# Feed-forward input stage: result banks and product banks of PSUM swap roles from block to block, weights split 2048 columns at a time, seven products at the 3rd and 6th pair

## The chip, the cores and the metric

The kernel runs on one core of a Trainium2 chip. Five engines work side by side, each through its own list of instructions in order: TensorE (PE, and PEld for the loading of its stationary operand), VectorE (DVE), ScalarE (ACT), GpSimd (POOL) and SyncE (SP), which here issues nearly all DMAs. Matrix products are summed in PSUM, eight banks of 128 partitions x 512 float32 values. The metric is the device time of one execution in microseconds (us); a run is the median of repeated executions.

## What is computed

One decoder layer for 256 tokens of width 2048: projections, two attention mixers, gates, an output product and a LayerNorm, then a feed-forward layer and a second LayerNorm. The change acts in the first half of the feed-forward layer, and in the names of the tiles elsewhere:

```python
FFN_HIDDEN = 5632

def _swiglu(h, w_ffn_in, w_ffn_out):
    g, u = jnp.split(h @ w_ffn_in, 2, axis=-1)
    return (jax.nn.silu(g) * u) @ w_ffn_out

h = _layer_norm(DEEPNORM_ALPHA * h + mix, ln1_g, ln1_b)
h = _layer_norm(DEEPNORM_ALPHA * h + _swiglu(h, w_ffn_in, w_ffn_out), ln2_g, ln2_b)
```

## The kernel before, in words

Every float32 operand is split into two parts of type float32r, a high one and a low rest (`split`, L70: a cast on ACT at L71, then a subtraction on DVE at L72), and each product is made of three matmuls (`mm3`, L90 to L93): high by high, high row by low weight, low row by high weight. Weights come in tiles of 128 x 2048 (1 MB, one DMA, three buffers called `raw`) and are split in halves of 1024 columns into two rings of eight buffers, `wh` and `wl`.

The feed-forward input product, h @ w_ffn_in, goes in 11 blocks `j` of 512 gate columns and 512 up columns. Block 0 is made in another way. Blocks 1 to 10 are made by `pair_product`: the 2048 rows of the weight are taken in eight pairs of 128-row tiles, and a pair is one `raw_fp` tile with four pieces of 512 columns (b11, b21 for the gate, b22, b12 for up). An ordinary pair gives 24 matmuls into four result banks, c11, c12, c21, c22 (gate and up, for the first and the second 128 tokens; in the trace `acc_fg` and `acc_fu`). In blocks 1 to 9 two of the pairs, those in `SEVEN`, are made by a Strassen-Winograd scheme: seven products instead of eight, so 21 matmuls. The first nine need the pieces b11, b21, b22 split (`whfp_2g`, `whfp_2u` and so on); the other twelve need four sums and differences of the pieces, which DVE makes in place (L737 to L740) and which are then split again (`whfp_2t`). Four of the seven products are shared between results and are summed in four further banks, `ps_` (`p` in the trace).

A scheduler sets the order of instructions on each engine from its own estimate of times; what each engine waits for follows from that order, since every engine works through its list in turn. The PSUM pool has two tags of four banks, `acc` and `tmp`. Before the change the four results of every block are `acc` and the four shared products are `tmp`. At the end of block j DVE adds shared products and results (L758 to L761) into SBUF, ACT and DVE form silu(gate) * up (L774, L775, L787), and two transposes on DVE write `rt` (L264). Eight steps later `move_blocks` (L286) copies `rt` to `act` with 16 DMAs of 32 x 256, issued by SP, the engine that also issues the `raw_fp` loads (L697). The first result bank of block j+1 is the bank that the add at L758 reads.

A `raw_fp` tile is free for a later load when its last split is done: the load of a pair takes the buffer of the pair three places earlier.

Of the kernel before, what the change touches and what calls it, by code (L numbers as in the profile page):

```python
# [17 lines left out]
P = 128  # L18
# [11 lines left out]
N = 512  # L30
# [14 lines left out]
def decoder_block(ctx, tc, xT, x, wz, lam_qk, subln, wa, wb, wo, g1, b1, b1T, wf, wfp, wfo, g2, b2,  # L45
# [24 lines left out]
    def split(src, hi, lo, eng=None):  # L70
        nc.scalar.copy(hi, src)  # L71
        (eng or nc.vector).tensor_sub(lo, src, hi)  # L72


    def split_weights(part, name, eng=None):
        wh = wp.tile([P, 2, N], F32R, tag="wh", name="wh" + name)
        wl = wp.tile([P, 2, N], F32R, tag="wl", name="wl" + name)
        split(part.rearrange("p (a n) -> p a n", n=N), wh, wl, eng)
        return wh, wl

    def weights(src, name, loads=1, pool=()):
        raw = wp.tile([P, 2048], F32, tag="raw", name="raw_" + name, bufs=3)
# [88 lines left out]
    def weights_and_x(src, name):  # L171
        c = int(name.split("_")[-1])
        for i in range(2):
            k0 = 4 * c + 2 * i
            raw = wp.tile([P, 2, N], F32, tag="raw", name="raw%d_%s" % (i, name), bufs=3)
            sv = src[:, i * 1024:(i + 1) * 1024].rearrange("p (a n) -> p a n", n=N)
            if k0 == 0:
                wh = wp.tile([P, 2, N], F32R, tag="wh", name="whf")
                wl = wp.tile([P, 2, N], F32R, tag="wl", name="wlf")
                xss = []  # L180
                for a in range(2):
                    xss.append(x_part(a, 1))
                    nc.sync.dma_start(raw[:, a, :], sv[:, a, :])
                for a in range(2):
                    split_x(xss[a], a, 1)
                    split(raw[:, a, :], wh[:, a, :], wl[:, a, :])
                yield wh, wl
            else:
                xs = x_part(k0, 2)
                nc.sync.dma_start(raw, sv)  # L190
                split_x(xs, k0, 2)
                yield split_weights(raw.rearrange("p a n -> p (a n)"), "%d_%s" % (i, name))
# [477 lines left out]

    SEVEN = (2, 4)
    forms = []

    def row_forms():
# [22 lines left out]

    def halves(src, name):  # L700
        n = src.shape[1]
        wh = wp.tile([P, 2, N], F32R, tag="wh", name="wh" + name)
        wl = wp.tile([P, 2, N], F32R, tag="wl", name="wl" + name)
        split(src, wh[:, 0:n], wl[:, 0:n])
        return [(wh[:, a, :], wl[:, a, :]) for a in range(n)]


    def pair_product(j):
        nk = KD // 2
        seven = SEVEN if j < NB_F - 1 else ()  # L710
        c11, c12, c21, c22 = [acc("acc_f%s_%d" % (c, j)) for c in ("g0", "u0", "g1", "u1")]
        ps_ = {}
        for i in range(nk):
            nm = "fp%d_%d" % (j, i)
            raw = load_pair(j, i)
            k0, k1 = 2 * i, 2 * i + 1
            first, final = i == 0, i == nk - 1
            if i not in seven:
                b11, b21 = halves(raw[:, 0:2], nm + "g")
                b22, b12 = halves(raw[:, 2:4], nm + "u")  # L720
                for ac, m, w0, w1 in ((c11, 0, b11, b21), (c12, 0, b12, b22), (c21, 1, b11, b21), (c22, 1, b12, b22)):
                    mm3(ac, *stat_h(m, k0), *w0, first, False)
                    mm3(ac, *stat_h(m, k1), *w1, False, final)
                tick()
                tick()
                continue
            n = seven.index(i)
            s0, s1 = n == 0, n == len(seven) - 1
            if s0:
                for f in (1, 6, 7, 5):  # L730
                    ps_[f] = tmp("p%d_%d" % (f, j))
            b11, b21 = halves(raw[:, 0:2], nm + "g")
            b22, = halves(raw[:, 2:3], nm + "u")
            mm3(ps_[1], *stat_h(0, k0), *b11, s0, s1)
            mm3(c11, *stat_h(0, k1), *b21, False, False)
            mm3(c12, *stat_s(4, n), *b22, False, False)
            nc.vector.tensor_sub(raw[:, 2], raw[:, 2], raw[:, 3])  # L737
            nc.vector.tensor_sub(raw[:, 3], raw[:, 3], raw[:, 0])
            nc.vector.tensor_add(raw[:, 0], raw[:, 2], raw[:, 0])
            nc.vector.tensor_sub(raw[:, 1], raw[:, 1], raw[:, 0])  # L740
            t2, t4 = halves(raw[:, 0:2], nm + "t2")
            t3, t1 = halves(raw[:, 2:4], nm + "t3")
            tick()
            mm3(ps_[6], *stat_s(2, n), *t2, s0, s1)
            mm3(ps_[7], *stat_s(3, n), *t3, s0, s1)
            mm3(ps_[5], *stat_s(1, n), *t1, s0, s1)
            mm3(c21, *stat_h(1, k1), *t4, False, False)
            tick()
            if s1:
                p1, u2, u3, t = [scr("%s_%d" % (c, j)) for c in ("p1", "u2", "u3", "u4")]  # L750
                nc.scalar.copy(p1, ps_[1])
                nc.vector.tensor_add(u3, p1, ps_[6])
                nc.vector.tensor_add(u2, u3, ps_[7])
                nc.vector.tensor_add(u3, u3, ps_[5])
                nc.vector.tensor_add(t, u2, ps_[5])
# [234 lines left out]
```

## Time and profile before

| what | value |
|---|---|
| time, median of 3 runs | 1380.2 us (1379.7 to 1380.85) |
| the profiled execution, its own time | 1384.11 us |
| its span, first to last instruction | 1382.3 us |
| granted TensorE clock, mean | 0.998 |
| PE busy | 1365.0 us, 99% of the span |
| DVE busy | 916.9 us, 66% |
| ACT busy | 644.5 us, 47% |
| DMA mean rate | 202 GB/s |

The busy share of PE counts a matmul from its start to its modelled end, and matmuls overlap: a 128 x 512 matmul lasts 0.39 us in the timeline, while the next one starts 0.23 us after it. Whether PE loses time is therefore read from the distances between starts, and from the time that a block of equal work takes. Below, T stands for the start of the first matmul of a block, and all times in a block are counted from it.

### The profile page before, as it was taken

The page shows a single profiled execution, that of the slowest core. Times are in us where ns is not written, and L with a number is a line of the kernel's source. Part 1 is how long each engine was busy: PE and PEld are TensorE (multiplying, and loading weights), DVE is VectorE, ACT ScalarE, POOL GpSimd, SP SyncE. Part 2 cuts the span into 40 slices and gives each one's busy share as a digit, 9 for nine tenths or more (in the row PEclk, how much of TensorE's full clock was granted, in tenths as well). Part 3 has the DMA queues.
Part 4 walks back from the last instruction along what each step waited for, and adds up shares of the span by engine and source line. Part 5 has one row for each costly group of instructions (what it writes and reads, how often), then busy time and mean ns, then how long its engine had stood idle before and what let it go on. Part 6 is the DMA issues. An engine that isn't in the chain of part 4 may idle for free.

```text
span 1382.3 us, 16276 instructions
## 1 busy us (share of the span) xinstructions
PE 1365.0 (99%) x6110; PEld 1126.0 (81%) x6110; DVE 916.9 (66%) x1161; ACT 644.5 (47%) x866; POOL 57.2 (4%) x64
## 2 busy tenths in 40 slices
PE   8999999999999999999999999999999999999997
PEld 6888888888888888888888888888788788888886
DVE  6666566766645454575878888888787765554555
ACT  4463444546444434443644455445454444444441
POOL 0001010100000000100000000000000000000003
PEclk9999999999999999999999999999999999999999
DMA  8583645464454649663445664546745676555541
GB/s 281 192 302 145 223 166 198 179 217 152 156 225 162 249 138 356 221 244 122 161 161 192 248 244 182 195 171 247 254 170 195 230 280 225 206 186 191 205 152 61
DMA packets 57151, 279.45 MB, mean 202 GB/s; under 512 B 10224, under 2 KB 22640, under 8 KB 25712
## 3 DMA queue, kind: packets, MB, share of 16 engines
q1 hardware_dynamic: 56784, 278.08, 55.2%
q8 instruction: 48, 0.79, 0.2%
q10 hardware_dynamic: 288, 0.33, 0.1%
q14 instruction: 31, 0.25, 0.1%
HBM read 264.74 MB, written 2.10 MB: 193 GB/s over the span
## 4 chain that ended last, share of the span: by engine, by line
PE 79%; DVE 9%; DMA 7%; ACT 2%; issue 2%; SPq 1%; POOL 0%; POOLq 0%; ACTq 0%; DVEq 0%
PE oacc L91 6%; PE oacc L93 6%; PE oacc L92 6%; DMA raw_fp<-in_wfp 5%; PE acc_fu L91 3%; PE acc_fu L93 3%; PE acc_fu L92 3%; PE acc_fg L91 3%; PE acc_fg L93 3%; PE acc_fg L92 3%; PE acc_gA L91 2%; PE acc_gB L93 2%; PE acc_gA L93 2%; PE acc_gA L92 2%; PE acc_gB L92 2%; PE acc_gB L91 2%
## 5 line engine op out<-in xcount | busy, mean ns | idle before, releaser
L72 DVE TENSOR_TENSOR wl_fo<-raw_fo,wh_fo 128x1024 fp32r<-128x1024 f32 x84 | 102.5, 1225 | 98.5 <-ACT wh_fo L71 93.4
L71 ACT CAST wh_fo<-raw_fo 128x1024 fp32r<-128x1024 f32 x84 | 88.2, 1055 | 115.4 <-PE oacc L93 99.2
L93 PE MATMUL oacc<-wh_fo,ahl 128*128 128x512 f32 x332 | 129.3, 389 | 0.0
L91 PE MATMUL oacc<-wh_fo,ahl 128*128 128x512 f32 x332 | 129.2, 389 | 0.0
L92 PE MATMUL oacc<-wl_fo,ahl 128*128 128x512 f32 x332 | 129.2, 389 | 0.0
L93 PEld LDWEIGHTS oacc<-wh_fo,ahl 128*128 128x128 f32 x332 | 62.3, 188 | 13.4 <-DVE ahl L72 0.3
L91 PEld LDWEIGHTS oacc<-wh_fo,ahl 128*128 128x128 f32 x332 | 62.3, 188 | 12.9
L92 PEld LDWEIGHTS oacc<-wl_fo,ahl 128*128 128x128 f32 x332 | 62.3, 188 | 12.9
L72 DVE TENSOR_TENSOR wl_gA<-raw_gA,wh_gA 128x1024 fp32r<-128x1024 f32 x32 | 38.9, 1220 | 35.9 <-ACT wh_gA L71 35.7
L72 DVE TENSOR_TENSOR wl_o<-raw_o,wh_o 128x1024 fp32r<-128x1024 f32 x32 | 39.5, 1235 | 33.9 <-ACT wh_o L71 33.9
L71 ACT CAST wh_gA<-raw_gA 128x1024 fp32r<-128x1024 f32 x32 | 33.6, 1054 | 53.3 <-PE acc_brB L93 20.0
L71 ACT CAST wh_o<-raw_o 128x1024 fp32r<-128x1024 f32 x32 | 33.7, 1054 | 48.5 <-PE acc_o L93 33.9
L72 DVE TENSOR_TENSOR wl_gB<-raw_gB,wh_gB 128x1024 fp32r<-128x1024 f32 x32 | 38.6, 1222 | 19.9 <-ACT wh_gB L71 19.3
L91 PE MATMUL acc_o<-wh_o,mth 128*128 128x512 f32 x128 | 50.4, 394 | 0.0
L91 PE MATMUL acc_gA<-wh_gA,xth 128*128 128x512 f32 x128 | 50.2, 392 | 0.0
L91 PE MATMUL acc_gB<-wh_gB,xth 128*128 128x512 f32 x128 | 50.1, 391 | 0.0
L93 PE MATMUL acc_o<-wh_o,mtl 128*128 128x512 f32 x128 | 49.9, 390 | 0.0
L92 PE MATMUL acc_o<-wl_o,mth 128*128 128x512 f32 x128 | 49.8, 389 | 0.0
L93 PE MATMUL acc_gB<-wh_gB,xtl 128*128 128x512 f32 x128 | 49.8, 389 | 0.0
L92 PE MATMUL acc_gA<-wl_gA,xth 128*128 128x512 f32 x128 | 49.8, 389 | 0.0
L92 PE MATMUL acc_gB<-wl_gB,xth 128*128 128x512 f32 x128 | 49.8, 389 | 0.0
L93 PE MATMUL acc_gA<-wh_gA,xtl 128*128 128x512 f32 x128 | 49.8, 389 | 0.0
(515 smaller groups left out, 3761.9 us busy)
## 6 DMA issues: line engine op xcount, KB each, us to landing
raw_fp<-in_wfp SPq DMA_DIRECT2D x80, 1024.0 KB, 5.9
raw_fo<-in_wfo SPq DMA_DIRECT2D x44, 1024.0 KB, 4.8
raw_gA<-in_wz SPq DMA_DIRECT2D x16, 1024.0 KB, 4.9
raw_gB<-in_wz SPq DMA_DIRECT2D x16, 1024.0 KB, 5.0
raw_o<-in_wo SPq DMA_DIRECT2D x16, 1024.0 KB, 4.8
raw_vA<-in_wz SPq DMA_DIRECT2D x8, 1024.0 KB, 5.1
raw_qB<-in_wz SPq DMA_DIRECT2D x8, 1024.0 KB, 6.9
raw_kB<-in_wz SPq DMA_DIRECT2D x8, 1024.0 KB, 5.2
```

The lines of the kernel that those rows point to most:

```text
L71: nc.scalar.copy(hi, src)
L72: (eng or nc.vector).tensor_sub(lo, src, hi)
L91: nc.tensor.matmul(ac, xh, wh, start=start, stop=False)
L92: nc.tensor.matmul(ac, xh, wl, start=False, stop=False)
L93: nc.tensor.matmul(ac, xl, wh, start=False, stop=stop)
```

## The change

Three things change in `pair_product`, and the tiles are renamed to suit:

- The banks change roles. In odd blocks the results take `acc` and the shared products `tmp`, in even blocks the other way round. The results of block j+1 so take the banks of the shared products of block j, and the shared products of block j+1, first used at pair 2, the banks of the results of block j.
- A pair is split by one cast and one subtraction of 2048 columns (1536 for the first three pieces of a pair by seven products), not in halves. The rings `wh` and `wl` of eight buffers of 1024 columns become one ring `w` of eight buffers of 2048 columns; an operation takes two of them, one for the high and one for the low parts. In the other stages one buffer of `w` holds the high and the low half of 1024 columns, as a buffer of each ring did before.
- `SEVEN` goes from (2, 4) to (2, 5): the 3rd and 6th pair instead of the 3rd and 5th.

```diff
     def split_weights(part, name, eng=None):
-        wh = wp.tile([P, 2, N], F32R, tag="wh", name="wh" + name)
-        wl = wp.tile([P, 2, N], F32R, tag="wl", name="wl" + name)
-        split(part.rearrange("p (a n) -> p a n", n=N), wh, wl, eng)
-        return wh, wl
+        w = wp.tile([P, 4, N], F32R, tag="w", name="w" + name)
+        split(part.rearrange("p (a n) -> p a n", n=N), w[:, 0:2], w[:, 2:4], eng)
+        return w[:, 0:2], w[:, 2:4]
...
-    SEVEN = (2, 4)
+    SEVEN = (2, 5)
...
     def halves(src, name):
         n = src.shape[1]
-        wh = wp.tile([P, 2, N], F32R, tag="wh", name="wh" + name)
-        wl = wp.tile([P, 2, N], F32R, tag="wl", name="wl" + name)
+        wh = wp.tile([P, 4, N], F32R, tag="w", name="wh" + name)
+        wl = wp.tile([P, 4, N], F32R, tag="w", name="wl" + name)
         split(src, wh[:, 0:n], wl[:, 0:n])
         return [(wh[:, a, :], wl[:, a, :]) for a in range(n)]
...
-        c11, c12, c21, c22 = [acc("acc_f%s_%d" % (c, j)) for c in ("g0", "u0", "g1", "u1")]
+
+        acc_c, acc_p = (acc, tmp) if j % 2 else (tmp, acc)
+        c11, c12, c21, c22 = [acc_c("acc_f%s_%d" % (c, j)) for c in ("g0", "u0", "g1", "u1")]
...
-                b11, b21 = halves(raw[:, 0:2], nm + "g")
-                b22, b12 = halves(raw[:, 2:4], nm + "u")
+                b11, b21, b22, b12 = halves(raw, nm)
...
-                    ps_[f] = tmp("p%d_%d" % (f, j))
-            b11, b21 = halves(raw[:, 0:2], nm + "g")
-            b22, = halves(raw[:, 2:3], nm + "u")
+                    ps_[f] = acc_p("p%d_%d" % (f, j))
+            b11, b21, b22 = halves(raw[:, 0:3], nm)
...
-            t2, t4 = halves(raw[:, 0:2], nm + "t2")
-            t3, t1 = halves(raw[:, 2:4], nm + "t3")
+            t2, t4, t3, t1 = halves(raw, nm + "t")
```

Outside the blocks 1 to 10 and the first loads behind them no engine's instructions change places. Inside them three places matter. The first is DVE around the end of a block, here block 4: `p1`, `u3`, `u2`, `u4` are the sums that read the result banks, `sl4` is silu, `rt4` the transposed block, `fp5_2` the weights of pair 2 of block 5. Before:

```order
L72 TENSOR_TENSOR wlfp5_2g_6932<-raw_fp5_2_6925,whfp5_2g_6931 128x1024
L72 TENSOR_TENSOR wlfp5_2u_6936<-raw_fp5_2_6925,whfp5_2u_6935 128x512
L758 TENSOR_TENSOR p1_4_6727<-p1_4_6727,acc_fg0_4_6515 128x512
L737 TENSOR_TENSOR raw_fp5_2_6925<-raw_fp5_2_6925 128x512
L759 TENSOR_TENSOR u3_4_6729<-u3_4_6729,acc_fu0_4_6516 128x512
L775 TENSOR_TENSOR sl4_0_6842<-sl4_0_6842,p1_4_6727 128x512
L738 TENSOR_TENSOR raw_fp5_2_6925<-raw_fp5_2_6925 128x512
L760 TENSOR_TENSOR u2_4_6728<-u2_4_6728,acc_fg1_4_6517 128x512
L787 TENSOR_TENSOR sl4_0_6842<-sl4_0_6842,u3_4_6729 128x512
L761 TENSOR_TENSOR u4_4_6730<-u4_4_6730,acc_fu1_4_6518 128x512
L775 TENSOR_TENSOR sl4_1_6845<-sl4_1_6845,u2_4_6728 128x512
L264 STREAM_TRANSPOSE rt4_6848<-sl4_0_6842 128x4x4x32
```

After the change, the same place:

```order
L756 TENSOR_TENSOR p1_4_6373<-p1_4_6373,acc_fg0_4_6159 128x512
L72 TENSOR_TENSOR wlfp5_1_6494<-raw_fp5_1_6491,whfp5_1_6493 128x2048
L757 TENSOR_TENSOR u3_4_6375<-u3_4_6375,acc_fu0_4_6160 128x512
L758 TENSOR_TENSOR u2_4_6374<-u2_4_6374,acc_fg1_4_6161 128x512
L759 TENSOR_TENSOR u4_4_6376<-u4_4_6376,acc_fu1_4_6162 128x512
L773 TENSOR_TENSOR sl4_0_6446<-sl4_0_6446,p1_4_6373 128x512
L773 TENSOR_TENSOR sl4_1_6449<-sl4_1_6449,u2_4_6374 128x512
L785 TENSOR_TENSOR sl4_0_6446<-sl4_0_6446,u3_4_6375 128x512
L785 TENSOR_TENSOR sl4_1_6449<-sl4_1_6449,u4_4_6376 128x512
L263 STREAM_TRANSPOSE rt4_6452<-sl4_0_6446 128x4x4x32
L263 STREAM_TRANSPOSE rt4_6452<-sl4_1_6449 128x4x4x32
L72 TENSOR_TENSOR wlfp5_2_6528<-raw_fp5_2_6521,whfp5_2_6527 128x1536
```

The splits of pair 2 of the next block stood ahead of the sums and now stand behind the transposes.

The second place is SP at the same block end, where the 16 moves of `rt4` stand between two loads. Before:

```order
L697 DMA raw_fp5_3_6972<-in_wfp 128x2048
L697 DMA raw_fp5_4_7022<-in_wfp 128x2048
L286 DMA act2_6514<-rt4_6848 32x256 x16
L697 DMA raw_fp5_5_7074<-in_wfp 128x2048
L697 DMA raw_fp5_6_7108<-in_wfp 128x2048
```

After the change:

```order
L696 DMA raw_fp5_3_6560<-in_wfp 128x2048
L696 DMA raw_fp5_4_6606<-in_wfp 128x2048
L285 DMA act2_6158<-rt4_6452 32x256 x16
L696 DMA raw_fp5_5_6636<-in_wfp 128x2048
L696 DMA raw_fp5_6_6680<-in_wfp 128x2048
```

Nothing moved here: the load of pair 5 is the first behind the moves in both, and pair 5 is now one of the two by seven products.

The third place is ACT in block 5, the casts of pairs 4 and 5 (a name that ends in t is of the sums and differences). Before:

```order
L71 CAST whfp5_4g_7024<-raw_fp5_4_7022 128x1024
L71 CAST whfp5_4u_7028<-raw_fp5_4_7022 128x512
L71 CAST whfp5_4t2_7045<-raw_fp5_4_7022 128x1024
L71 CAST whfp5_4t3_7049<-raw_fp5_4_7022 128x1024
L71 CAST whfp5_5g_7076<-raw_fp5_5_7074 128x1024
L71 CAST whfp5_5u_7080<-raw_fp5_5_7074 128x1024
```

After the change, from pair 2 on:

```order
L71 CAST whfp5_2t_6544<-raw_fp5_2_6521 128x2048
L71 CAST whfp5_3_6562<-raw_fp5_3_6560 128x2048
L71 CAST whfp5_4_6608<-raw_fp5_4_6606 128x2048
L71 CAST whfp5_5_6638<-raw_fp5_5_6636 128x1536
L71 CAST whfp5_5t_6655<-raw_fp5_5_6636 128x2048
```

The second cast of a pair by seven products moved from pair 4 to pair 5, and each piece of work is one instruction where it was two.

## Rows read from the trace of the kernel before

**Rows 1.** The page, part 1: engine, busy us (share of the span), instructions.
```profile
PE 1365.0 (99%) x6110; PEld 1126.0 (81%) x6110; DVE 916.9 (66%) x1161; ACT 644.5 (47%) x866; POOL 57.2 (4%) x64
```
**Rows 2.** Busy time by stretch, one block from T to T each: blocks 4, 7, 8, 9.
```profile
core 0: us, PE busy (x) PEld busy (x) DVE busy (x) ACT busy (x) POOL busy (x), PEclk, DMA share, GB/s
...
831.74:873.90 42.16, 42.16 (x188) 34.91 (x186) 35.12 (x42) 20.93 (x23) 0.00 (x0) 1.00 0.56 212
...
958.22:1001.89 43.67, 42.32 (x187) 34.75 (x186) 34.91 (x41) 20.18 (x23) 0.00 (x0) 1.00 0.60 210
1001.89:1044.83 42.94, 42.69 (x187) 34.76 (x187) 35.73 (x43) 20.68 (x24) 0.00 (x0) 1.00 0.54 208
1044.83:1088.24 43.41, 42.64 (x186) 34.76 (x187) 35.12 (x42) 21.10 (x24) 0.00 (x0) 1.00 0.62 224
```
**Rows 3.** Waits of PE: who waited for whom, us in total, times, longest.
```profile
PE acc_fg L91 <- DVE p L758: 2.4, 3, 1.4
```
**Rows 4.** Timeline of PE at the end of block 7: start, duration, instruction [idle before].
```profile
1000.15 0.39 PE L93 MATMUL acc_fu<-whfp_7u,htl 128*128 128x512 f32 x1
1001.89 0.47 PE L91 MATMUL acc_fg<-whfp_0g,hth 128*128 128x512 f32 x1 [1.35 <-DVE p L758]
1002.20 0.40 PE L92 MATMUL acc_fg<-wlfp_0g,hth 128*128 128x512 f32 x1
```
**Rows 5.** Timeline of DVE at the end of block 7.
```profile
999.32 1.23 DVE L72 TENSOR_TENSOR wlfp_2g<-raw_fp,whfp_2g 128x1024 fp32r<-128x1024 f32 x1 [2.56 <-ACT whfp_2g L71]
1000.47 0.68 DVE L72 TENSOR_TENSOR wlfp_2u<-raw_fp,whfp_2u 128x512 fp32r<-128x512 f32 x1
1001.07 0.68 DVE L758 TENSOR_TENSOR p<-p,acc_fg 128x512 f32<-128x512 f32 x1
```
**Rows 6.** Timeline of DVE behind the start of block 5 (T = 873.90).
```profile
875.42 0.68 DVE L761 TENSOR_TENSOR u<-u,acc_fu 128x512 f32<-128x512 f32 x1
876.02 0.69 DVE L775 TENSOR_TENSOR sl<-sl,u 128x512 f32<-128x512 f32 x1
876.62 0.71 DVE L264 STREAM_TRANSPOSE rt<-sl 128x512 f32<-128x512 f32 x1
877.25 0.65 DVE L787 TENSOR_TENSOR sl<-sl,u 128x512 f32<-128x512 f32 x1
```
**Rows 7.** SP's issues in blocks 5 and 6, and line L286 over the span (ns min/median/max).
```profile
879.15 10.01 SPq L286 DMA_DIRECT2D act<-rt  x16
889.26 4.82 SPq L697 DMA_DIRECT2D raw_fp<-in_wfp  x3
...
921.17 11.03 SPq L286 DMA_DIRECT2D act<-rt  x16
...
L286 SPq DMA_DIRECT2D act<-rt x176: 507/589/1592, 709.7 to 1144.2; - x176
```
**Rows 8.** Timeline of ACT in block 5.
```profile
883.66 1.06 ACT L71 CAST whfp_4g<-raw_fp 128x1024 fp32r<-128x1024 f32 x1
885.03 0.62 ACT L71 CAST whfp_4u<-raw_fp 128x512 fp32r<-128x512 f32 x1 [0.32 <-PE acc_fu L93]
890.27 2.00 ACT L71 CAST whfp_4t<-raw_fp 128x1024 fp32r<-128x1024 f32 x2 [4.62 <-DVE raw_fp L740]
894.46 1.05 ACT L71 CAST whfp_5g<-raw_fp 128x1024 fp32r<-128x1024 f32 x1 [2.19 <-DMA raw_fp<-in_wfp]
```
**Rows 9.** Timeline of DVE in block 5, the pair by seven products.
```profile
885.44 1.22 DVE L72 TENSOR_TENSOR wlfp_4g<-raw_fp,whfp_4g 128x1024 fp32r<-128x1024 f32 x1
886.57 0.68 DVE L72 TENSOR_TENSOR wlfp_4u<-raw_fp,whfp_4u 128x512 fp32r<-128x512 f32 x1
887.29 0.69 DVE L737 TENSOR_TENSOR raw_fp<-raw_fp 128x512 f32<-128x512 f32 x1
...
889.47 0.69 DVE L740 TENSOR_TENSOR raw_fp<-raw_fp 128x512 f32<-128x512 f32 x1
891.36 2.36 DVE L72 TENSOR_TENSOR wlfp_4t<-raw_fp,whfp_4t 128x1024 fp32r<-128x1024 f32 x2 [1.20 <-ACT whfp_4t L71]
```

More of the change, by code (lines that the diff above doesn't have):

```diff
@@ L177, in weights_and_x @@
             if k0 == 0:
-                wh = wp.tile([P, 2, N], F32R, tag="wh", name="whf")
-                wl = wp.tile([P, 2, N], F32R, tag="wl", name="wlf")
+                w = wp.tile([P, 4, N], F32R, tag="w", name="wf")
+                wh, wl = w[:, 0:2], w[:, 2:4]
                 xss = []
```

## The prediction

> **What bounds the kernel now.** I read the busy shares first: PE is at 99% [rows 1], so time is to be had only where PE waits or works slower. Then a block of the feed-forward input by itself: a block of equal work takes 42.16 us where nothing disturbs it, for 6 x 24 + 2 x 21 = 186 matmuls, or 0.2267 us from start to start, at a granted clock of 1.00 [rows 2]. That is the floor, and the change does not touch it, since the number of matmuls stays. Three blocks take longer: 43.67, 42.94 and 43.41, together 3.54 us over the floor [rows 2]. The waits of PE name the cause: three times it waits for the add at L758 [rows 3]. At the end of block 7 the next matmul starts 1.74 us after the last one instead of 0.23 [rows 4]; it needs the bank that L758 reads, and L758 stands on DVE behind the splits of pair 2 of the next block, which waited 2.56 us for their cast [rows 5]. So a late weight load delays a sum, and the sum delays PE.
>
> The second thing to see is how little room the other engines have inside a block: DVE is busy 35 of 42 us [rows 2]. What counts there is when a particular split is done, so I follow one chain through the block, from T, the start of its first matmul.
>
> **The banks.** With the roles swapped, the first result bank of a block is one that held a shared product of the block before. Its last reader is a sum that DVE makes after the second pair by seven products, while PE still has pairs 6 and 7 to do, 48 matmuls or 10.9 us. In the new order of DVE two splits of 2048 columns stand near these sums, about 2.3 us each by the estimate below, so the banks are free some 5 us early. The banks of the results are wanted again only at pair 2, 10.9 us into the next block. The three waits go: -3.5 us. If a wait remained it would be no longer than now, so the bounds are -3.5 and 0.
>
> **The wide splits.** None is in the trace, so I take durations along the line of the narrow ones: a cast takes 0.62 us for 512 columns and 1.06 for 1024 [rows 8], which gives 1.48 for 1536 and 1.92 for 2048; a subtraction takes 0.68 and 1.22 [rows 9], which gives 1.76 and 2.30. Side by side, two narrow subtractions of 1024 take 2.36 us [rows 9], so a wide one saves 0.06, a narrow cast pair takes 2.00 [rows 8], saving 0.08. A block has ten fewer on each engine: below 1 us of DVE and of ACT, on engines that are not the bound, so nothing of it reaches the end by itself. From below the bound is a gain of zero; what it may cost is latency: the first piece of a split is ready after 1.92 + 2.30 us where it was ready after 1.06 + 1.22, about 1.9 us later, and matters only where PE waits for that piece.
>
> The Trainium skill ("VectorE: DVE Perf Modes", section "The TRN2 errata — SBUF-src ops pay a fixed extra latency per instruction") says that one large tile pays the fixed latency once where many small ones pay it each, and gives (N + 151) / 0.96 ns for a float32 subtraction, 2.29 us at 2048 columns. The rule speaks for the change; by it each merged pair would save 0.16 us of DVE, 1.6 us a block, where the trace leaves 0.06 since neighbours overlap; were DVE the bound, nine blocks would gain 14 us by the rule and 5 by the row. It says nothing of when the first piece is ready.
>
> **The 6th pair, and the 16 moves ahead of it.** Here is the price. SP works in order: the load of pair 5 stands behind the 16 moves of the block just finished, before as after. It is the first load behind them, so its time follows from the block's start:
> - The last matmul of a block starts 0.23 us before T and lasts 0.39 [rows 4], so the last sum can start at T + 0.2. In the new order it, four products of silu and two transposes follow each other. Neighbours on DVE start 0.60 apart, a transpose takes 0.63 until the next may start and 0.71 itself [rows 6]: 0.2 + 5 x 0.60 + 0.63 + 0.71 = T + 4.55 for the end of the second transpose, on which the first move waits.
> - 16 moves take 10.01 us in block 5 and 11.03 in block 6, and the load follows at once: 879.15 to 889.26, or 10.1 [rows 7]. One move in a train can take 1.59 us instead of 0.59 [rows 7]; I take half of the trains at 10.1 and half at 11.1, 10.6 on average: T + 15.15.
> - From its issue to the first cast the load of pair 5 needs 889.26 to 894.46 [rows 7, 8], 5.2 us: T + 20.35. In block 5 that is 894.46 - 873.90 = T + 20.6 today, which agrees.
> - Then the chain that a pair by seven products has and an ordinary one has not. Cast of 1536 columns 1.48 and hand-over 0.04 (890.27 + 1.05 against 891.36 [rows 8, 9]), subtraction 1.76 and 0.04, four sums in place until the next cast 890.27 - 887.29 = 2.98 [rows 8, 9], cast of 2048 1.92 and 0.04, subtraction 2.30 and 0.04. Sum 10.6: the low parts of the sums are ready at T + 30.95.
> - PE wants them at the second matmul of the second part of pair 5. Ahead of it stand 24 + 24 + 21 + 24 + 24 + 9 + 1 = 127 matmuls, T + 28.8.
>
> PE waits 2.15 us there, and 0.08 for the restart (0.31 to the next matmul instead of 0.23 [rows 4]): 2.2 us. Today pair 5 is ordinary, its splits are done some 2.5 us after its cast starts and PE wants it after 114 matmuls, at T + 25.8, so the same late load is covered by nearly 3 us. The old second pair, pair 4, has its load ahead of the moves. The 2.2 us come back in each block, since moves, load and chain all start from the new T. They fall in blocks 2 to 9; block 1 has no sums ahead of its transposes, which frees the moves about 2 us earlier, and I count it as 0 (bounds 0 and 1). So 8 x 2.2 = +17.6 us. Bounds: with every train at 10.1 and a little less on the load, 1.5 a block or 12 us; with every train at 11.1 and half a microsecond more on the load, 3.2 or 26 us.
>
> At pair 2 the chain starts behind the transposes: 4.5 + 1.8 + 2.98 + 1.96 + 2.34 = T + 13.6, wanted at (48 + 9 + 1) matmuls = T + 13.15. That wait of about 0.4 us is not added, because it moves PE, not the load of pair 5, and shortens the wait there by as much.
>
> **The sum.** -3.5 + 17.6 = +14.1 us. The profiled execution took 1384.11 us, 1.8 of it outside the span, and lies 3.9 above the median 1380.2; the difference is made within one execution and carried to the median: 1394.3, said as 1394.
>
> **The rivals.**
> - *The waits go and nothing comes in their place.* For it: the three waits are plain in the trace, and DVE and ACT have fewer instructions. Against it: the chain above is 2.15 us too long, and every link but the two widths is measured. It decides if the load of pair 5 has landed by T + 18.2, or the chain of 10.6 takes 8.4. Time: 1380.2 - 3.5 = 1376.7. Chance 0.12. By the rule of the Trainium skill above ("VectorE: DVE Perf Modes") it would go this way, since fewer and larger splits only save time.
> - *The two cancel.* The chain is 1.7 to 2 us shorter than I make it, so that PE waits 0.2 to 0.7 us a block: 1380.2 - 3.5 + 8 x 0.45 = 1380. Chance 0.08.
> - *The lateness spreads.* The load of pair 0 of the next block takes the buffer of pair 5 and can be issued only at T + 31; with 5.2 for the load, 1.96 and 2.34 it is ready at T + 40.5, wanted at 42.2 + 2.2 = T + 44.4. From 3.9 us more on one of these loads PE would wait there too; at 1 to 2 us a block that is 8 to 16 on top, 1402 to 1410. The trace speaks against it: no load there is that late. Chance 0.07.
> - *The change does not do what it says.* The sums that free the shared products' banks stand behind splits that wait for the late load of pair 7, and the waits at block starts stay: 1394.3 + 3.5 = 1398. Against it stand the 5 us above. Chance 0.03.
> - *The forecast*, slower by 10 to 20 us: chance 0.70.
>
> **How the numbers follow.** The range should take in the bounds of the 17.6 us, 12 to 26, hence 1389 to 1403, and reaches down to the cancelling case: 1380 to 1403. Left out are the first rival, most of the third and half of the second. A measurement of this kernel tells about 0.2% from no change, 2.8 us. Faster by more: the first rival, 0.12. Within: the second, 0.08. Slower: the rest, 0.80.
>
> **What would show it.** Right: the waits of PE no longer name a sum at a block's first matmul; they name a cast or split of the second part of pair 5, some 2 us, eight times; a block from T to T takes 44.2 to 44.6 us; the load of pair 5 is issued about T + 15. Wrong: blocks of 42.2 us, or a wait at another pair, or a load of pair 5 issued before T + 13.

## The result, and the profile after

| what | before | after |
|---|---|---|
| median in the same comparison | 1380.53 us | 1402.99 us (four runs, 1400.18 to 1407.4) |
| ratio | | 1.0163, 95% interval 1.0131 to 1.0196 |
| the profiled execution, its own time / its span | 1384.11 / 1382.3 us | 1405.04 / 1403.2 us |
| granted TensorE clock, mean | 0.998 | 0.994 |

The change makes the kernel slower by 22.5 us on the medians, and by 20.9 from one profiled execution to the other. DVE and ACT have fewer instructions and PE is still nearly always busy, as the page of after says, part 1 (the line that answers to [rows 1]):

```profile
PE 1372.9 (98%) x6110; PEld 1128.8 (80%) x6110; DVE 912.1 (65%) x1063; ACT 631.2 (45%) x768; POOL 57.3 (4%) x64
```

The waits of PE in after (who waited for whom, us in total, times, longest) answer to [rows 3]. The sum at the start of a block is gone from the list; the second part of pair 5 (`5t`) has taken its place, and pair 2 stands there too:

```profile
PE p L91 <- DVE wlfp_5t L72: 11.8, 8, 1.8
PE p L90 <- ACT whfp_5t L71: 2.3, 2, 1.5
PE p L91 <- DVE wlfp_2t L72: 1.8, 3, 0.8
```

Busy time by stretch, blocks 1 to 6 of after from T to T (stretch, its length, then the engines, and after them the granted clock, PEclk), to be held against [rows 2]:

```profile
704.64:746.80 42.16, 42.16 (x187) 34.91 (x186) 28.08 (x22) 18.15 (x11) 0.00 (x0) 1.00 0.52 189
746.80:795.47 48.67, 44.62 (x188) 35.89 (x186) 36.30 (x35) 20.20 (x14) 0.00 (x0) 0.96 0.50 185
795.47:842.43 46.96, 44.34 (x188) 35.94 (x186) 35.00 (x33) 19.47 (x13) 0.00 (x0) 0.96 0.49 188
842.43:886.76 44.33, 42.67 (x188) 34.76 (x187) 35.50 (x33) 19.58 (x13) 0.00 (x0) 1.00 0.55 202
886.76:930.60 43.84, 42.66 (x187) 34.76 (x186) 35.40 (x33) 19.50 (x13) 0.00 (x0) 1.00 0.55 204
930.60:976.77 46.17, 44.34 (x188) 35.91 (x186) 35.41 (x33) 19.47 (x13) 0.00 (x0) 0.96 0.52 194
```

Block 1 is on the floor of 42.16 us, no other is, and three of them (2, 3, 6) show a lower mean clock. From the distances between the starts of neighbouring matmuls I split what each block has above the floor into the waits at pair 2, the waits at pair 5 (both with their restart), and the stretches in which matmuls stand 0.43 us apart where it should be 0.227:

| block | 2 | 3 | 4 | 5 | 6 | 7 | 8 | 9 | sum |
|---|---|---|---|---|---|---|---|---|---|
| above 42.16 us | 6.51 | 4.80 | 2.17 | 1.69 | 4.01 | 1.67 | 2.06 | 2.69 | 25.6 |
| at pair 5 | 3.96 | 3.36 | 1.93 | 1.45 | 2.33 | 1.35 | 1.31 | 1.60 | 17.3 |
| at pair 2 | 0.96 | 0 | 0.19 | 0.19 | 0.20 | 0.20 | 0.63 | 1.05 | 3.4 |
| slow matmuls | 1.55 | 1.40 | 0 | 0 | 1.40 | 0 | 0 | 0 | 4.35 |

The 3.54 us of the kernel before come off. The rest is small: block 1 starts 0.6 us earlier, and what follows block 9 is 0.6 shorter. 25.6 - 3.5 - 0.6 - 0.6 = 20.9, the difference of the spans.

**One block's chain.** Block 5 of after, T = 886.76, in the timeline (start, duration, engine, instruction, idle time before it and what ended it). SP, with the 16 moves and the load of pair 5 at their heels:

```profile
891.30 10.01 SPq L285 DMA_DIRECT2D act<-rt  x16
901.41 3.51 SPq L696 DMA_DIRECT2D raw_fp<-in_wfp  x3
```

DVE: the transposes, the last split of pair 2, then pair 5 (first split, last of the four sums, second split):

```profile
889.97 1.30 DVE L263 STREAM_TRANSPOSE rt<-sl 128x512 f32<-128x512 f32 x2
...
897.86 2.29 DVE L72 TENSOR_TENSOR wlfp_2t<-raw_fp,whfp_2t 128x2048 fp32r<-128x2048 f32 x1 [2.05 <-ACT whfp_2t L71]
...
908.03 1.76 DVE L72 TENSOR_TENSOR wlfp<-raw_fp,whfp 128x1536 fp32r<-128x1536 f32 x1 [3.47 <-ACT whfp L71]
...
912.00 0.69 DVE L739 TENSOR_TENSOR raw_fp<-raw_fp 128x512 f32<-128x512 f32 x1
914.75 2.29 DVE L72 TENSOR_TENSOR wlfp_5t<-raw_fp,whfp_5t 128x2048 fp32r<-128x2048 f32 x1 [2.06 <-ACT whfp_5t L71]
```

ACT, the two casts of pair 5, and PE, the first two matmuls of its second part:

```profile
906.52 1.48 ACT L71 CAST whfp<-raw_fp 128x1536 fp32r<-128x1536 f32 x1 [5.06 <-DMA raw_fp<-in_wfp]
912.80 1.91 ACT L71 CAST whfp_5t<-raw_fp 128x2048 fp32r<-128x2048 f32 x1 [4.81 <-DVE raw_fp L739]
...
915.53 0.39 PE L90 MATMUL p<-whfp_5t,formshl 128*128 128x512 f32 x1
917.10 0.50 PE L91 MATMUL p<-wlfp_5t,formshl 128*128 128x512 f32 x1 [1.18 <-DVE wlfp_5t L72]
```

The transposes end at T + 4.51, the load is issued at T + 14.65, the cast starts at T + 19.76, the low parts are ready at 914.75 + 2.29 = T + 30.28. PE wanted them 0.23 after 915.53 and gets them 1.34 us late. A second thing stands in these rows: pair 2's last split ends at 897.86 + 2.29 = 900.15, and pair 5 is loaded into the buffer that this split sets free (three buffers, pairs 2 and 5). In this block the moves hold the load 1.2 us longer than the buffer does, no more.

### The profile page after: what moved, and what is told of

Its sections match the earlier page's. It is cut to its first block, busy times and chain, and to the rows that moved or that the text cites. A ratio compares the mean times of both kernels' runs of the same rounds, so it can differ in the third digit from the quotient of the medians.

```text
span 1403.2 us, 15970 instructions
## 1 busy us (share of the span) xinstructions
PE 1372.9 (98%) x6110; PEld 1128.8 (80%) x6110; DVE 912.1 (65%) x1063; ACT 631.2 (45%) x768; POOL 57.3 (4%) x64
## 4 chain that ended last, share of the span: by engine, by line
PE 76%; DVE 9%; DMA 6%; SPq 4%; ACT 3%; issue 2%; POOL 0%; POOLq 0%; ACTq 0%; DVEq 0%
PE oacc L91 6%; PE oacc L92 6%; PE oacc L90 6%; DMA raw_fp<-in_wfp 4%; SPq L285 3%; DVE wlfp L72 2%; PE acc_fg L90 2%; PE acc_fg L91 2%; PE acc_fg L92 2%; PE acc_gA L90 2%; PE acc_gB L92 2%; PE acc_gA L92 2%; PE acc_gA L91 2%; PE acc_gB L91 2%; PE acc_gB L90 2%
## 5 line engine op out<-in xcount | busy, mean ns | idle before, releaser
L72 DVE TENSOR_TENSOR wlfp<-raw_fp,whfp 128x2048 fp32r<-128x2048 f32 (+1 forms) x80 | 172.1, 2164 | 63.8 <-ACT whfp L71 61.5
L71 ACT CAST whfp<-raw_fp 128x2048 fp32r<-128x2048 f32 (+1 forms) x80 | 144.0, 1812 | 129.7 <-DMA raw_fp<-in_wfp 104.5
L72 DVE TENSOR_TENSOR w_fo<-raw_fo,w_fo 128x1024 fp32r<-128x1024 f32 x84 | 102.2, 1224 | 95.9 <-ACT w_fo L71 91.3
L91 PE MATMUL oacc<-w_fo,ahl 128*128 128x512 f32 x332 | 129.2, 389 | 0.0
L90 PE MATMUL oacc<-w_fo,ahl 128*128 128x512 f32 x332 | 129.1, 389 | 0.0
L92 PE MATMUL oacc<-w_fo,ahl 128*128 128x512 f32 x332 | 129.0, 389 | 0.0
L90 PE MATMUL acc_fg<-whfp,hth 128*128 128x512 f32 x266 | 103.7, 390 | 0.0
L91 PE MATMUL acc_fg<-wlfp,hth 128*128 128x512 f32 x266 | 103.7, 390 | 0.0
L92 PE MATMUL acc_fg<-whfp,htl 128*128 128x512 f32 x266 | 103.6, 389 | 0.0
L91 PE MATMUL acc_fu<-wlfp,hth 128*128 128x512 f32 x248 | 96.5, 389 | 0.0
L92 PE MATMUL acc_fu<-whfp,htl 128*128 128x512 f32 x248 | 96.5, 389 | 0.0
L90 PEld LDWEIGHTS oacc<-w_fo,ahl 128*128 128x128 f32 x332 | 62.3, 188 | 13.1
L92 PEld LDWEIGHTS oacc<-w_fo,ahl 128*128 128x128 f32 x332 | 62.2, 188 | 13.0 <-DVE ahl L72 0.2
L91 PEld LDWEIGHTS oacc<-w_fo,ahl 128*128 128x128 f32 x332 | 62.3, 188 | 12.9
L92 PEld LDWEIGHTS acc_fg<-whfp,htl 128*128 128x128 f32 x266 | 50.1, 188 | 10.4
```

The lines of the kernel that those rows point to most:

```text
L90: nc.tensor.matmul(ac, xh, wh, start=start, stop=False)
L91: nc.tensor.matmul(ac, xh, wl, start=False, stop=False)
L92: nc.tensor.matmul(ac, xl, wh, start=False, stop=stop)
```

## The experiments

All kernels compute the whole layer. Where block lengths are given they are read as above.

**Each part alone, and both without the third.** The bank roles alone:

```diff
-        c11, ... = [acc("acc_f%s_%d" % (c, j)) ...]
+        acc_c, acc_p = (acc, tmp) if j % 2 else (tmp, acc)
+        c11, ... = [acc_c("acc_f%s_%d" % (c, j)) ...]
-                    ps_[f] = tmp("p%d_%d" % (f, j))
+                    ps_[f] = acc_p("p%d_%d" % (f, j))
```

> The kernel before with the swap of bank roles alone; halves of 1024 columns and the pairs (2, 4) stay. Theory (the loss comes from pair 5 standing behind the 16 moves, the swap by itself only takes the three block-start waits away): 1376.5 to 1377.5 us, no wait of TensorE for a sum at a block's first matmul, blocks 4 to 9 at 42.2 us, granted clock 0.998 or more. Rival 1 (the swap is what costs, by holding a bank longer than the prediction says): 1385 us or more, with a wait at the shared products' first matmul in pair 2 or at a block's start.

Measured: 1381.14 us, ratio 0.9989 (0.9970 to 1.0007). All of the blocks 1 to 9 take 42.16 us: the three waits go, as the theory has it, but the time does not fall to the expected 1377: the ratio gives 1.5 us less, the two medians of this comparison 0.7, and the interval includes no change. The widths alone (`halves` and `split_weights` as in the change, shown in part):

```diff
-                b11, b21 = halves(raw[:, 0:2], nm + "g")
-                b22, b12 = halves(raw[:, 2:4], nm + "u")
+                b11, b21, b22, b12 = halves(raw, nm)
```

> The kernel before with splits of 2048 columns alone; old bank roles, pairs (2, 4). Theory (the widths are worth nothing by themselves, the block-start waits stay or go with the order of VectorE): 1377 to 1382 us. Rival (wide splits delay the sums that free the result banks by another microsecond): waits of 1 to 2 us at each block's start, 1386 to 1395 us.

Measured: 1380.02 us, 0.9989 (0.9979 to 1.0000), again all nine blocks at 42.16 us. The waits at block starts go with this edit alone as well, so it is not shown that the swap is what removes them in the change. The whole change with the pairs put back:

```diff
-    SEVEN = (2, 5)
+    SEVEN = (2, 4)
```

> The changed kernel with the seven products put back to pairs 2 and 4; swapped banks and wide splits stay. Theory (it takes pair 5 behind the moves for the loss): the load of pair 4 stands ahead of the moves, so no wait at the second part of a late pair, clock 0.998 or more, 1376 to 1379 us. Rival 3 (the widths cost by themselves, wherever the pairs are): waits at pair 2 and pair 4 of 1 to 2 us a block, 1390 us or more.

Measured: 1379.91 us, 0.9985 (0.9976 to 0.9995), the lowest ratio of this study; its interval overlaps those of the two parts. Block 9, one of the three in which the kernel before lost time [rows 2], by stretch as above:

```profile
1041.98:1084.14 42.16, 42.16 (x188) 34.92 (x186) 35.42 (x32) 19.87 (x13) 0.00 (x0) 1.00 0.59 217
```

So banks and widths are worth about 2 us, and the whole loss, some 24 us, comes with the pairs (2, 5). The four kernels of this study that have every block on the floor (these three, and the one at pairs 3 and 5 below) have spans from 1377.6 to 1380.1 us; their blocks begin at 704.7 to 707.2 us, so that spread is made ahead of the blocks.

**The pairs alone, and the pairs with narrow splits.** The old kernel with pair 5:

```diff
-    SEVEN = (2, 4)
+    SEVEN = (2, 5)
```

> The kernel before with seven products at pairs 2 and 5 alone; halves of 1024 columns and the old bank roles stay. Theory: the load of pair 5 is late as in the changed kernel, but its chain is made of narrow pieces; from first cast to the first low parts of the sums it takes about 8.9 us instead of 10.6, and the transposes end a microsecond earlier, so the wait at the second part of pair 5 is 0 to 1 us a block and the three block-start waits stay: 1380 to 1388 us. Rival 2 (the place of pair 5 costs by itself, whatever the widths): 2 us a block as in the changed kernel, 1395 us or more. Rival 3 (the place costs nothing, all of the loss is from the widths): 1380 us and no wait at pair 5.

Measured: 1398.91 us, 1.0118 (1.0103 to 1.0133). My theory fell, and the time is the one that rival 2 names: the chain is shorter by 2.3 us (from the first cast to the first low parts of the sums 8.2 us in block 5, where after has 10.52), and yet blocks 3 to 9 wait 1.7 to 2.7 us at pair 5, for the transposes end at T + 6.5 to 7.2 and the load is issued at T + 16.7 to 18.1. The waits at block starts, expected to stay, are gone here too but for 0.2 us at the end of block 5. With the banks swapped as well (the change with halves of 1024 columns, shown in part):

```diff
-            b11, b21, b22 = halves(raw[:, 0:3], nm)
+            b11, b21 = halves(raw[:, 0:2], nm + "g")
+            b22, = halves(raw[:, 2:3], nm + "u")
```

> The changed kernel with halves of 1024 columns again; swapped banks and the pairs (2, 5) stay. The run with pairs (2, 5) alone had narrow halves too and was 16 us slower, with its transposes ending 6.5 us after a block's start instead of 4.5, since splits stood ahead of the sums. Theory (two things make pair 5 late: when the transposes end, and what stands ahead of its load; the widths add 1.7 us of chain): if the sums come first, as in the changed kernel, the wait is 0 to 0.7 us a block and the time 1377 to 1383 us; if the splits come first, 2 to 2.7 us a block and 1393 to 1400 us. Rival (the widths make the loss): 1380 us at most in either order.

Measured: 1396.42 us, 1.0104 (1.0088 to 1.0121), the second branch of the theory. DVE in block 6 of this kernel, T = 923.25: two splits of pair 2 stand among the sums and ahead of the second transpose.

```profile
922.52 1.22 DVE L72 TENSOR_TENSOR wlfp_2g<-raw_fp,whfp_2g 128x1024 fp32r<-128x1024 f32 x1
923.65 0.68 DVE L760 TENSOR_TENSOR u<-u,acc_fu 128x512 f32<-128x512 f32 x1
...
928.45 0.68 DVE L72 TENSOR_TENSOR wlfp_2u<-raw_fp,whfp_2u 128x512 fp32r<-128x512 f32 x1
929.05 0.70 DVE L264 STREAM_TRANSPOSE rt<-sl 128x512 f32<-128x512 f32 x1
```

Within this one kernel the link from transposes to wait can be seen. In blocks 2 and 5 they end at T + 4.2 and 5.2, the load is issued at T + 15.4 in both, and PE loses 0.5 us at pair 5; in the six others they end at 6.5 to 6.7, the load is issued at 16.7 to 17.3, and PE loses 2.0 to 2.8. Against this kernel the change takes 6 to 8 us more (6.6 between the medians, 8 by the ratios): that is what the wide splits cost with pairs (2, 5), together with the other order that they bring on DVE. With pairs (2, 4) they cost nothing.

**What makes pair 5 late.** First the moves, given to GpSimd:

```diff
-                nc.sync.dma_start(dst[32 * b:32 * b + 32, i], rt[32 * i:32 * i + 32, b])
+                nc.gpsimd.dma_start(dst[32 * b:32 * b + 32, i], rt[32 * i:32 * i + 32, b])
```

> The changed kernel with the 16 moves of each block issued by GpSimd instead of SyncE; nothing else is edited. Theory (the load of pair 5 waits on SyncE behind the moves): the load is issued as soon as its buffer is free, some 8 us earlier, the waits at pair 5 go in all eight blocks, and with them the three stretches at a granted clock of 0.5: 1376 to 1379 us. Rival 4 (the load is late because its buffer comes free late, or because the transfers are slow): the load stays where it is and the time stays at 1400 us. Rival 5 (the clock falls by themselves, whatever TensorE waits for): the waits go, the falls stay, 1381 us or more.

Measured: 1392.06 us, 1.0070 (1.0055 to 1.0085). Half of the loss goes, not all. The blocks lose 10.2 us in total, 7.4 at pair 2 and 2.2 at pair 5; no block has slow matmuls. Two things stand in the trace of block 5, T = 876.61, in its rows of DVE and SP:

```profile
875.65 0.68 DVE L756 TENSOR_TENSOR p<-p,acc_fg 128x512 f32<-128x512 f32 x1
876.24 1.75 DVE L72 TENSOR_TENSOR wlfp<-raw_fp,whfp 128x1536 fp32r<-128x1536 f32 x1
877.91 0.68 DVE L757 TENSOR_TENSOR u<-u,acc_fu 128x512 f32<-128x512 f32 x1
...
888.22 2.29 DVE L72 TENSOR_TENSOR wlfp_2t<-raw_fp,whfp_2t 128x2048 fp32r<-128x2048 f32 x1 [2.06 <-ACT whfp_2t L71]
...
890.53 4.73 SPq L696 DMA_DIRECT2D raw_fp<-in_wfp  x3
```

The load of pair 5 is issued at 890.53, right when the last split of pair 2 is done (888.22 + 2.29 = 890.51): rival 4 holds for the load once the moves are out of its way. That is T + 13.92 in place of 14.65. And the split of pair 2 has moved in among the sums, so the transposes end at T + 6.8 to 7.4, pair 2 is late, and PE waits there. How much the moves alone would give in an unchanged order on DVE is not shown, since the scheduler set another order with them. Next the buffer: the long pairs (2, 6), where pair 6 takes the buffer of pair 3 and still loads behind the moves.

```diff
-    SEVEN = (2, 5)
+    SEVEN = (2, 6)
```

> The changed kernel with the seven products at pairs 2 and 6 in place of 2 and 5. With three buffers pair 5 takes the buffer of pair 2, and in the run with the moves on GpSimd its load started right when the last split of pair 2 was done, some 14 us into the block. Pair 6 takes the buffer of pair 3 and is still loaded behind the moves. Theory A (pair 5 is bad since it has both the moves and the buffer of the other long pair against it): load of pair 6 at 15.8 us, its second low parts at 31.5, wanted at 34.2: no wait, 1376 to 1380 us, granted clock 0.998. Theory B (any long pair behind the moves costs): 1 to 2 us a block, 1385 to 1395 us.

Measured: 1393.00 us, 1.0078 (1.0063 to 1.0093). Neither theory names the place. PE hardly waits at pair 6; it waits at pair 2 and at what follows it:

```profile
PE acc_fg L90 <- ACT whfp L71: 4.2, 7, 0.6
PE p L90 <- ACT whfp_2t L71: 2.5, 6, 0.6
```

Pair 1 of the next block takes the buffer of pair 6 and is loaded at T + 35.5 where it was T + 32.5, pair 2 comes behind it, and its cast is made 1.2 us into its own block (block 5), where after has it 2.2 us ahead of the block. The lateness of the loads spreads into the next block, a rival of the prediction that had been tied to pair 5. What pair 2 waits for last in block 5 is DVE, T = 876.91: a split of pair 1 stands among the sums, the transposes end at T + 7.07, and the split of pair 2, cast by T + 2.7, starts behind them.

```profile
878.07 2.29 DVE L72 TENSOR_TENSOR wlfp<-raw_fp,whfp 128x2048 fp32r<-128x2048 f32 x1
...
882.67 1.30 DVE L263 STREAM_TRANSPOSE rt<-sl 128x512 f32<-128x512 f32 x2
883.89 1.72 DVE L72 TENSOR_TENSOR wlfp<-raw_fp,whfp 128x1536 fp32r<-128x1536 f32 x1
```

How much of the loss is the late loads and how much the other order on DVE is not shown. Then both obstacles of pair 5 taken away at once, with a long pair still in the same late place:

```diff
-    SEVEN = (2, 5)
+    SEVEN = (3, 5)
```

> The changed kernel with the seven products at pairs 3 and 5 in place of 2 and 5. Pair 5 stays the second long pair and is wanted at the same time, 28.8 us into the block, but its buffer is now that of pair 2 as an ordinary pair, whose one split is done early, and the scheduler has its load ahead of the 16 moves. Theory A (pair 5 is late in the changed kernel since its load stands behind the moves and in the buffer of the other long pair): the load is issued before the moves, no wait at pair 5, pair 6 behind the moves is covered as an ordinary pair: 1376 to 1380 us. Theory B (a long pair as late in the block as the 6th costs for itself, by the work on VectorE and ScalarE that it puts there): waits of 1.5 us or more a block at pair 5, 1390 us or more. A third way is that the splits which the order now has ahead of the second transpose hold pair 3 up: waits at pair 3 of about 1 us, 1385 to 1390 us.

Measured: 1379.53 us, 0.9988 (0.9974 to 1.0001), all nine blocks at 42.16 us. SP around T = 875.81: two loads, the second that of pair 5, now stand ahead of the moves.

```profile
873.16 4.57 SPq L696 DMA_DIRECT2D raw_fp<-in_wfp  x2
883.23 10.02 SPq L285 DMA_DIRECT2D act<-rt  x16
893.35 11.88 SPq L696 DMA_DIRECT2D raw_fp<-in_wfp  x4
```

The low parts of pair 5 are ready at T + 26.9, wanted at 28.8, though the transposes end as late as T + 7.4. A long pair in that place costs nothing when its load is early. Theory A is shown for the two obstacles together; apart, the rows of block 5 above give the buffer's bound (T + 13.4) and the moves' (T + 14.65). Last, more moves: four of the 16 made twice.

```diff
-        for i in range(4):
+        for i in (0, 1, 2, 3, 3):
```

> The changed kernel with 20 moves in place of 16 behind each block: four of them are made twice. The order of instructions on TensorE, ScalarE and VectorE in the blocks is that of the changed kernel, so only the load of pair 5 gets later, by 4 x 0.63 = 2.5 us. Theory A (the load behind the moves sets the wait): the wait at the second part of pair 5 grows by 2.5 us in each of the blocks 2 to 9, to some 4 to 5 us, block 1, which had no wait and some 1 us to spare, gets 1 to 2 us, and a longer wait is followed by a fall of the clock in nearly each block, 1.6 us apiece: 1403 + 8 x 2.5 + 1.5 + 5 to 8 = 1430 to 1433 us. Theory B (the buffer of pair 2 sets it, and the moves are hidden): less than half of that, 1403 to 1415 us.

Measured: 1414.82 us, 1.0244 (1.0227 to 1.0262), by its number at the top of theory B's range, but the dose was not the one I meant. SP in block 5, T = 887.98:

```profile
892.52 10.65 SPq L285 DMA_DIRECT2D act<-rt  x17
903.27 0.53 SPq L696 DMA_DIRECT2D raw_fp<-in_wfp  x1
903.89 1.77 SPq L285 DMA_DIRECT2D act<-rt  x3
```

The scheduler put one added move ahead of the load and three behind it. The load goes 0.64 us later (T + 15.29 for 14.65), it takes 5.5 us to the cast in place of 5.1, and the low parts are 1.0 later (T + 31.30 for 30.28). The waits at pair 5 grow from 17.3 to some 24.4 us, the slow matmuls from 4.35 to 7.4 (five falls of the clock for three), block 1 stays at 42.16. So the wait follows the load, as theory A has it, at a smaller dose than its sum assumed.

**The clock.** The changed kernel again, nothing edited:

> The changed kernel once more, nothing edited, for a second profile and four more times. Theory A (the falls follow from the waits in blocks 2, 3 and 6, which the order of the instructions makes long): 1400 to 1407 us again, the same long blocks 2 and 3, and two to four falls in the blocks. Theory B (the falls and the long blocks are chance): other blocks are long, or none.

Measured: 1402.41 us, 1.0151 (1.0132 to 1.0171). In this profile the blocks lose 21.2 us: 16.4 at pair 5, 1.7 at pair 2, 2.6 in slow matmuls, all of these in block 2. Block 2 is long again (49.33), block 3 much less (44.04). So the waits come back, and the falls of the clock only in part (one, of double length): waits of 2.27 and 2.28 us from start to start, in blocks 6 and 4, were not followed by one, while that of 2.25 in block 6 of the first profile was. Then waits put in on purpose into the kernel with pairs (2, 4), ahead of pair 5 and longer from block to block:

```diff
+    def hold(j, bank, pieces):
+        z = small("hold%d" % j)
+        nc.scalar.activation(z, bank[:, 0:4], AF.Copy, scale=0.0)
+        for _ in range(3 * (j - 1)):
+            nc.scalar.copy(z, z)
+        for w, _ in pieces:
+            nc.scalar.activation(w[:, 0:4], w[:, 0:4], AF.Identity, bias=z[:, 0:1])
...
+                if i == 5 and seven:
+                    hold(j, ps_[5], (b11, b21, b22, b12))
```

> The changed kernel with the seven products at pairs 2 and 4, whose blocks all run on the floor at a granted clock of 1.0, and one wait of TensorE put into each of the blocks 1 to 9, ahead of pair 5: a chain of small ScalarE operations that starts when a shared product is done and ends in the weights of pair 5, 3 operations longer from block to block, so that the waits grow from about 1 us to some 6 us. Theory A (a long wait is followed by a fall of the clock): the first blocks show no fall, from some block on each wait is followed by one stretch of 3.4 us at a granted clock of 0.5, and these blocks lose some 1.6 us more than their wait. Theory B (the falls in the changed kernel had nothing to do with the waits): the clock stays at 1.0 in the blocks, each loses its wait alone.

Measured: one run, 1459.18 us. The waits came out longer than meant, 3.5 us in block 1 and 4.9 to 7.7 in the others, and each of the nine was followed by slow matmuls, 11.8 us lost in all. Then a chain that starts at an earlier product:

```diff
-        for _ in range(3 * (j - 1)):
+        for _ in range(6 + 2 * j):
...
-                    hold(j, ps_[5], (b11, b21, b22, b12))
+                    hold(j, ps_[1], (b11, b21, b22, b12))
```

> As the kernel with one wait put into each block, pairs (2, 4), with a chain that starts at an earlier product and grows by two ScalarE operations of 0.22 us from block to block, so that the waits run from about 0.7 us in block 1 to 4 us in block 9. Theory A (what a fall follows is a long wait): no fall after the waits of the first three blocks, one of 3.41 us after each of the last four. Theory B (any wait can be followed by one): falls in the first blocks too.

Measured: one run, 1431.93 us. PE in blocks 3 and 4, the last matmul ahead of the wait and those behind it:

```profile
816.22 0.39 PE L92 MATMUL acc_fg<-whfp_4t,htl 128*128 128x512 f32 x1
817.81 0.50 PE L90 MATMUL acc_fg<-whfp,hth 128*128 128x512 f32 x1 [1.21 <-ACT whfp L713]
818.15 0.39 PE L91 MATMUL acc_fg<-wlfp,hth 128*128 128x512 f32 x1
...
859.88 0.39 PE L92 MATMUL acc_fg<-whfp_4t,htl 128*128 128x512 f32 x1
864.61 0.80 PE L90 MATMUL acc_fg<-whfp,hth 128*128 128x512 f32 x1 [4.34 <-ACT whfp L713]
865.21 0.63 PE L91 MATMUL acc_fg<-wlfp,hth 128*128 128x512 f32 x1
```

From start to start the wait is 1.6 us in block 3, 2.0 in block 2, and the clock stays at 1.00 in both; it is 4.4 to 7.7 in blocks 4 to 9, and each of these is followed by matmuls 0.43 us apart. The blocks lose 11.5 us to them. That a wait of 3.5 us or more brings the fall is shown (15 of 15, in one execution of each of these two kernels), and that a block with no wait has none (nine blocks each in four kernels). For shorter waits both outcomes are on record: in the kernel with 20 moves a wait of 2.33 us at pair 5 was followed by a fall in five blocks of eight, and in the kernel with narrow splits one fall came in block 4, behind two neighbouring waits of 1.16 and 1.26 us from start to start. What decides there stays open.

## Where the prediction was right, and which steps failed

- **The sign, the place and the mechanism were right.** The waits at block starts went and waits at the second part of pair 5 came, eight of them, none in block 1. With the pairs put back the loss is gone. The size was too small: 13.8 us forecast, 22.5 measured on the medians.
- **The banks, -3.5: right in the trace, too large for the median.** All three waits go, with the swap alone or with the widths alone. But the 3.5 us were read from an execution 3.9 us above its median; the swap alone is worth 0.7 us between the medians and 1.5 by the ratio, not told from zero by its interval.
- **The wide splits, about 0 by themselves: right** (0.9989, at most 0.2% faster). The durations were hit: 1.91 and 2.29 us for 2048 columns (1.92 and 2.30 estimated), 1.48 and 1.76 for 1536. By the Trainium skill ("VectorE: DVE Perf Modes", section "The TRN2 errata — SBUF-src ops pay a fixed extra latency per instruction") a float32 tensor_tensor operation of 2048 columns takes 2.29 us, and the trace agrees; that fewer and larger splits save time shows in DVE's busy time at most, not in the end.
- **The chain in a block, link by link, in block 5 of after.** Second transpose T + 4.51 (T + 4.55 forecast). Moves 10.0 in six of the eight blocks, not in half of them (10.4 in block 4, 10.8 in block 2): load at T + 14.65, not 15.15. Load to cast 5.1 (5.2). Cast to low parts 10.52 (10.6). Blocks 4 to 9 so lose 1.66 us each at pair 5 and 0.41 at pair 2, 2.07 together, where 2.2 were forecast.
- **The step that failed first: the sum has no term for the clock.** 4.35 us, three stretches of slow matmuls behind the longest waits. The profile before shows no fall in these blocks, but it shows no wait longer than 1.74 us either [rows 4]; the range should have had it.
- **The step that failed second: 8 equal blocks, sized by the order of block 5.** The term of 17.6 us holds what PE loses at pairs 2 and 5 together, since a wait at pair 2 comes off the one at pair 5. It measured 20.7 (17.3 and 3.4). Blocks 4 to 9 lose 12.4 instead of 13.2, blocks 2 and 3 lose 8.3 instead of 4.4; that the waits at pair 5 alone come to 17.3 is luck. In blocks 2 and 3 the split of pair 2 still stands ahead of sums, which the forecast took from the order of block 5 for all blocks. DVE at the start of block 2, T = 746.80:

```profile
745.87 1.76 DVE L72 TENSOR_TENSOR wlfp<-raw_fp,whfp 128x1536 fp32r<-128x1536 f32 x1 [0.41 <-ACT whfp L71]
747.55 0.68 DVE L756 TENSOR_TENSOR p<-p,acc_fg 128x512 f32<-128x512 f32 x1
...
752.35 1.30 DVE L263 STREAM_TRANSPOSE rt<-sl 128x512 f32<-128x512 f32 x2
```

  The transposes end at T + 6.85 and the load of pair 5 is issued at T + 17.76.
- **The wait at pair 2: rightly not added.** The forecast had 0.4 us there, to come off the wait at pair 5. It measured 0.2 in four blocks and up to 1.05 in block 9, and it does come off: in block 9, T = 1064.82, the transposes end at T + 5.36, the load is issued at T + 15.50, and the low parts of pair 5 are ready at 1093.82 + 2.29 = T + 31.29. That is 2.5 behind the T + 28.8 of the forecast, and the two waits, 1.05 and 1.60 with their restarts, make that up.

```profile
1093.82 2.29 DVE L72 TENSOR_TENSOR wlfp_5t<-raw_fp,whfp_5t 128x2048 fp32r<-128x2048 f32 x1 [2.05 <-ACT whfp_5t L71]
```

- **What the prediction did not see: pair 5's buffer.** It had the moves as the one thing ahead of the load. In block 5 of after the buffer of pair 2 comes free at T + 13.4, only 1.2 us before the moves let the load go. An estimate from the trace of after: with the load issued when the buffer is free, and the rest of each block's chain as measured, the low parts of pair 5 would be behind T + 28.8 by 4.6 us over the eight blocks (0.3 in block 5), where they are behind by 19.2. So the moves set about three quarters of the lateness and the buffer the rest, as long as the order on DVE stays.
- **The rivals.** That the lateness spreads is not what happened here; with pairs (2, 6) the loads of the next block do come later. That nothing takes the place of the waits is what (2, 4) and (3, 5) show.

Together: 14.1 forecast, plus 4.35 for the clock, 3.1 on the main term and 0.5 in small restarts, less 1.2 outside the blocks, gives 20.9, the difference of the profiled executions. The medians are 22.5 apart; the other 1.6 us are not accounted for by these two executions.

## What to carry to other kernels

A tile that needs a long chain before its use should not be the first load behind a train of small DMAs on the same issuing engine, nor share a ring's buffer with another such tile: with three buffers, two long tiles three places apart do. Another place is not free by that alone: with pairs (2, 6) the next block paid. A wait that is put into a loop is priced with what follows it, the slower matmuls after it, and over all turns of the loop, since a scheduler may order the first turns in another way than the later ones. And when a change has several parts, the one that moves work to a later deadline decides; here the other two were harmless with pairs (2, 4) and with (3, 5).

## What the runs showed of the hardware

TensorE's granted clock falls to 0.5, its level of 1.2 GHz, behind some of the waits in the middle of a kernel that otherwise runs at 1.00. PE in block 6 of after:

```profile
959.42 0.42 PE L90 MATMUL p<-whfp_5t,formshl 128*128 128x512 f32 x1
961.67 0.73 PE L91 MATMUL p<-wlfp_5t,formshl 128*128 128x512 f32 x1 [1.83 <-DVE wlfp_5t L72]
962.20 0.63 PE L92 MATMUL p<-whfp_5t,formshl 128*128 128x512 f32 x1
962.63 0.63 PE L90 MATMUL p<-whfp_5t,formshl 128*128 128x512 f32 x1
...
964.76 0.59 PE L92 MATMUL p<-whfp_5t,formshl 128*128 128x512 f32 x1
965.19 0.40 PE L90 MATMUL acc_fg<-whfp_5t,hth 128*128 128x512 f32 x1
```

Matmuls stand 0.43 us apart, seven of them, then 0.23 again: 1.4 us on top of a wait of 2 us. The Trainium skill ("TensorE: Matmul & The Clock Gate", section "Wait — 56ns, not 53.3ns?") gives 426.7 ns between 512-column matmuls at the lower level, and the trace agrees. Block 6 so lost 4.0 us where block 4, with a wait only 0.2 us shorter, lost 2.2. The other surprise is the moves: 16 DMAs of 32 KB hold SP for 10.0 us (block 5 of after) and GpSimd for 7.8 (the kernel with the moves there), longer than the 5.1 us that a load of 1 MB takes from issue to its first reader.
